# Output projection split in its own tiles, four homes for put-off residuals, and the second norm's root taken on 128x4 numbers

## The chip, the cores and the metric

One NeuronCore of a Trainium2 chip runs the whole program. The metric is device time in microseconds (us) of one execution; of several executions the median counts. The core has a matmul engine (PE, with its weight loads shown as PEld), a vector engine (DVE), an activation engine (ACT), a general engine (POOL, which here only issues DMAs) and SyncE (SP, which also issues DMAs). Each engine works through its own instructions in a fixed order and waits on semaphores of the others.

## The reference, cut to what matters

One layer of a decoder block over 2048 tokens of 1024 features. `g1`, `sh2`, `sc2`, `g2` are vectors made from the condition `c`.

```python
h = rms_norm(x, norm1_g) * (1 + sc1) + sh1
...  # gated linear attention (4 heads) and dilated attention (8 heads) on h
x = x + g1 * (concat(gla_out, attn_out) @ w_out)          # output projection
h = rms_norm(x, norm2_g) * (1 + sc2) + sh2                # the second norm
u = causal_depthwise_conv(h @ w_up, conv_w, conv_b)
a, b = split(u, 2)
x = x + g2 * ((silu(a) * b) @ w_down)                     # down projection

def rms_norm(x, g):
    return x * rsqrt(mean(x * x, axis=-1) + 1e-6) * g
```

## The kernel before

**Layout.** Tokens are cut into four chunks of T = 512 (c = 0 to 3). All activations lie with features on the 128 partitions and tokens along the row, so a chunk is KD = 8 tiles of 128x512. A matrix product is kept near fp32 by splitting both operands in a rounded part and a rest (`whi`, `wlo` for weights; `hhi`, `hlo` or `ghi`, `glo` for activations) and running three matmuls for each 128-block of the contraction (`mm3`: L314 hi·hi, L315 hi·lo, L316 lo·hi). Weights come by DMA on the POOL queue (L243) and are split by ACT (L248) and DVE (L249). GEMM results go to four PSUM banks (`psg`), everything else to the other four (`psa`).

**Order.** The program is traced by a tile framework whose scheduler, with an internal model of times, fixes the order on every engine. The source interleaves the mixing of chunk c+1 (`mix`: gated linear attention `gla`, then `attn` for four head pairs) with the GEMM chain of chunk c (`outproj(c)`, then `ffn(c)`); chunk 3's chain stands alone at the end.

**outproj(c).** The mixing has written its eight 128x512 results to DRAM, `y[0..7]` (`gla` the first four, `attn` of head pair hp the block 4+hp, L1051). `outproj` loads each back on the POOL queue into one of three "sq" tiles (L1067) and splits it (ACT L1076 hi, DVE L1077 lo). Eight column blocks follow (L1083 adds the residual and makes `x1`).

**Second norm.** ACT squares the eight `x1` tiles (L437), DVE adds them (L442). One fp32 matmul with a matrix of 1/1024 sums over partitions and spreads the mean over all of them (L456, 128x512). ACT takes Ln (L458) and Exp of -0.5 times it (L459), each with its own activation table; for chunk 0 four more DVE operations (L463 to L466) sharpen the root. Then for each feature block DVE multiplies (L476), ACT adds the shift and rounds (L478, `hhi`), DVE makes the rest (L480, `hlo`). The up-projection of `ffn` reads these.

**The put-off work.** Between the statistics and that last step `outproj` runs `self.tail`, GEMM work kept back so that PE is busy meanwhile. For c = 1 to 3 it is the last `down` group of the chunk before: eight column blocks of two 128-blocks, 48 matmuls. Each block reloads its residual from DRAM (L1148) into the tiles `y0` or `y1` (two slots each), adds (L1151) and stores (L1153 the result, L1155 the earlier partial `x1`). For c = 0 it is a piece of the input projection of chunk 3.

Of the kernel before, what the change touches and what calls it, by code (L numbers as in the profile page):

```python
# [10 lines left out]
F32 = mybir.dt.float32  # L11
# [3 lines left out]
ALU = mybir.AluOpType  # L15
# [129 lines left out]
class K:  # L145
# [174 lines left out]
    def ada_setup(self):  # L320
# [11 lines left out]
        self.eps = self.const.tile([P, 1], F32, name="eps")  # L332
        nc.vector.memset(self.eps, EPS)
        th = self.at.tile([P, 1024], F32, name="th", tag="v4", bufs=1)
        tanh = nc.scalar.activation(th, self.cond, AF.Tanh, scale=0.5)
# [88 lines left out]

    def norm_stats(self, src, step=False):

        acc = None
        for k in range(KD):
            acc = self.square(acc, src(k))
        return self.norm_end(acc, step)  # L430

# [12 lines left out]

    def norm_end(self, acc, step=False, split=False, more=()):
        nc = self.nc
# [12 lines left out]
        nc.scalar.activation(rstd, rstd, AF.Exp, scale=-0.5)  # L459
        if step:  # L460

            t = self.tmp.tile([P, T], F32, name="sq", bufs=3)
            nc.vector.scalar_tensor_tensor(t, ms, self.eps[:, 0:1], rstd, op0=ALU.add, op1=ALU.mult)  # L463
            nc.vector.tensor_tensor(t, t, rstd, op=ALU.mult)
            nc.vector.tensor_scalar(t, t, -3.0, -0.5, op0=ALU.add, op1=ALU.mult)
            nc.vector.tensor_tensor(rstd, rstd, t, op=ALU.mult)  # L466
        return rstd
# [200 lines left out]
    def gla(self, c, a):  # L668
# [106 lines left out]
        for s in range(2):  # L775
# [19 lines left out]
            yield  # L795
        nc.scalar.activation(ss, ss, AF.Ln, bias=self.eps, scale=1.0 / P)
        nc.scalar.activation(ss, ss, AF.Exp, scale=-0.5)
        ys = []
# [26 lines left out]
    def attn(self, c, hp, ready):  # L825
# [224 lines left out]
        nc.vector.tensor_tensor(st.rearrange("p (l r) -> p r l", r=16), O.rearrange("p (r l) -> p r l", r=16), st.rearrange("p (l r) -> p r l", r=16), op=ALU.add)  # L1050
        nc.sync.dma_start(D[c]["y"][4 + hp], st)  # L1051
        yield
# [9 lines left out]
    def outproj(self, c):  # L1062
        nc, A = self.nc, self.A
        hs = []
        for k in range(KD):
            t = self.tmp.tile([P, T], F32, name="sq", bufs=3)
            ld = self.dq.dma_start(t, self.D[c]["y"][k])  # L1067
            self.soon(ld)

            if c or k > 5:  # L1070
                hi, lo = (self.hp.tile([P, T], F32R, name=n) for n in ("hhi", "hlo"))
            elif k == 5:
                hi, lo = (self.up.tile([P, T], F32R, name=n, tag=n) for n in ("y0", "y1"))
            else:
                hi, lo = (self.gp.tile([P, T], F32R, name=n, tag=n) for n in ("ghi", "glo"))
            nc.scalar.copy(hi, t)  # L1076
            nc.vector.tensor_tensor(lo, t, hi.bitcast(F32), op=ALU.subtract)  # L1077
            hs.append((hi, lo))
        x1 = self.load_x(c)
        for cb in range(KD):  # L1080
            ps = self.pg()
            self.mm3(ps, self.weights("w_out", cb), hs)
            nc.vector.scalar_tensor_tensor(x1[cb], ps, self.mod[:, 16 + cb:17 + cb], x1[cb], op0=ALU.mult, op1=ALU.add)  # L1083
            yield
        self.x1[c] = x1
        rstd = self.norm_stats(lambda k: x1[k], not c)
        yield from self.tail
        self.h2[c] = self.norm_mod(lambda k: x1[k], rstd, self.G2, self.mod[:, 24:32], True)

# [43 lines left out]
    def down(self, c, gj, pgs):  # L1133
# [6 lines left out]
        for q in range(1024 // cols):  # L1140
            w = self.weights("w_down", gj * 4 + q)
            for cc in range(cols // P):
# [3 lines left out]
                if gj == 5 and defer:  # L1146
                    x1 = self.up.tile([P, T], F32, name="x1", tag=f"y{cb % 2}")
                    self.dq.dma_start(x1, self.D[c]["x1"][cb])  # L1148
# [182 lines left out]
```

## Time and profile before

| | |
|---|---|
| runs | 2580.99, 2582.28, 2589.22 us; median 2582.28 |
| profiled execution | 2578.59 us, of which the span of instructions is 2576.8 us |
| granted PE clock | 0.999 on average |
| busy, of the span | PE 2543.0 us, PEld 2096.0, DVE 1899.6, ACT 1264.6, POOL 449.2 |
| DMA | 408.47 MB, mean 159 GB/s |

The busy times show which engine the program leans on; the rows of single instructions show when each ran, how long it took, and behind "<-" in brackets what it had been waiting for. A waiting time is only worth something if PE is the engine that waits.

### The profile page before, as it was taken

Reading aid. Unit: us, or ns where it says so; the run is one execution under the profiler, and the core shown is the slowest. Engines: PE = TensorE matmul, PEld = TensorE weight load, DVE = VectorE, ACT = ScalarE, POOL = GpSimd, SP = SyncE. Lnnn points to the kernel's source line nnn. Section 1 sums busy time; section 2 is a strip of 40 time slices with the busy share of each in tenths; the row PEclk is TensorE's granted clock in tenths of the full one; section 3 lists DMA queues with packets and bytes.
Section 4 is the critical chain, followed back from the end, with each engine's and each line's share of the span. In section 5 each row is a group of like instructions: output and inputs, shape, how many; then the busy total and the mean of one; then the engine's idle time right before and its main releaser. Section 6 shows DMA issues by size and latency. Waiting matters only on the chain.

```text
span 2576.8 us, 49715 instructions
## 1 busy us (share of the span) xinstructions
PE 2543.0 (99%) x19458; PEld 2096.0 (81%) x19458; DVE 1899.6 (74%) x4111; ACT 1264.6 (49%) x2624; POOL 449.2 (17%) x818
## 2 busy tenths in 40 slices
PE   7999999999999999999999999999999999999999
PEld 4888888888788888887888888878888888788887
DVE  7678877867688766677977777689777775766665
ACT  5556655656454444454545444346444443433332
POOL 2333432323210000022100000310000003200001
PEclk9999999999999999999999999999999999999999
DMA  8876665756633444456334444743444535433232
GB/s 326 266 242 203 223 226 178 239 169 211 211 111 99 128 133 128 134 178 203 123 108 130 141 139 117 248 141 112 127 137 136 146 106 198 150 98 98 98 99 82
DMA packets 190622, 408.47 MB, mean 159 GB/s; under 512 B 48642, under 2 KB 89652, under 8 KB 189108
## 3 DMA queue, kind: packets, MB, share of 16 engines
q0 software_dynamic: 88416, 309.64, 37.0%
q1 hardware_dynamic: 101972, 95.65, 12.7%
q8 instruction: 154, 2.52, 0.4%
q14 instruction: 80, 0.66, 0.1%
HBM read 342.30 MB, written 62.91 MB: 157 GB/s over the span
## 4 chain that ended last, share of the span: by engine, by line
PE 94%; DVE 2%; issue 1%; DMA 1%; ACT 1%; POOL 1%; SPq 0%; POOLq 0%; DVEq 0%; ACTq 0%
PE psg L314 27%; PE psg L315 27%; PE psg L316 27%; PE psa L1028 2%; PE psa L902 2%; PE psa L876 2%; PE psa L709 2%; PE psa L1023 1%; PE psa L925 1%; PE psa L782 1%; PE psa L781 1%; PE psa L456 0%; PE psa L786 0%; PE psg L1200 0%; PE psa L1047 0%
## 5 line engine op out<-in xcount | busy, mean ns | idle before, releaser
L314 PE MATMUL psg<-hhi,whi 128*128 128x512 f32 x1968 | 771.2, 394 | 4.8 <-DVE x L1151 3.3
L315 PE MATMUL psg<-hlo,whi 128*128 128x512 f32 x1968 | 769.7, 392 | 2.2 <-DVE hlo L1077 1.9
L316 PE MATMUL psg<-hhi,wlo 128*128 128x512 f32 x1968 | 769.3, 392 | 0.7 <-DVE wlo L249 0.7
L248 ACT CAST whi<-wraw 128x1024 fp32r<-128x1024 f32 (+1 forms) x388 | 407.1, 1051 | 472.4 <-PE psg L315 360.7
L249 DVE TENSOR_TENSOR wlo<-wraw,whi 128x1024 fp32r<-128x1024 f32 (+1 forms) x388 | 474.5, 1223 | 202.7 <-ACT whi L248 194.4
L314 PEld LDWEIGHTS psg<-hhi,whi 128*128 128x128 f32 x1968 | 369.4, 188 | 84.9 <-ACT hhi L478 5.9
L316 PEld LDWEIGHTS psg<-hhi,wlo 128*128 128x128 f32 x1968 | 369.5, 188 | 78.6 <-DVE wlo L249 1.1
L315 PEld LDWEIGHTS psg<-hlo,whi 128*128 128x128 f32 x1968 | 369.6, 188 | 78.4 <-DVE hlo L1077 2.3
L314 PE MATMUL psg<-ghi,whi 128*128 128x512 f32 x744 | 294.6, 398 | 0.1
L315 PE MATMUL psg<-glo,whi 128*128 128x512 f32 x744 | 292.0, 393 | 0.4 <-DVE glo L1077 0.4
L316 PE MATMUL psg<-ghi,wlo 128*128 128x512 f32 x744 | 291.1, 391 | 0.7 <-DVE wlo L249 0.7
L243 POOL DMA_DIRECT2D wraw<-in_w_up_dram x176 | 96.4, 548 | 979.2 <-DVE wlo L249 814.8
L1151 DVE SCALAR_TENSOR_TENSOR x<-psg,mod,x 128x512 f32<-128x512 f32 x192 | 143.1, 748 | 112.4 <-PE psg L316 111.5
L314 PE MATMUL psg<-whi,hhi 128*128 128x512 f32 (+2 forms) x512 | 172.8, 342 | 2.9 <-ACT stg L582 1.4
L315 PE MATMUL psg<-wlo,hhi 128*128 128x512 f32 (+2 forms) x512 | 173.2, 339 | 0.0
L316 PE MATMUL psg<-whi,hlo 128*128 128x512 f32 (+2 forms) x512 | 173.0, 341 | 0.0
L314 PEld LDWEIGHTS psg<-ghi,whi 128*128 128x128 f32 x744 | 140.0, 188 | 31.3 <-issue 1.4
L316 PEld LDWEIGHTS psg<-ghi,wlo 128*128 128x128 f32 x744 | 139.9, 188 | 30.0 <-DVE wlo L249 1.1
L315 PEld LDWEIGHTS psg<-glo,whi 128*128 128x128 f32 x744 | 140.0, 188 | 28.9 <-DVE glo L1077 0.8
L1106 ACT ACTIVATE y<-psg,tables_sb 128x512 f32<-128x512 f32 x176 | 136.0, 775 | 3.0 <-PE psg L316 2.0
L1107 DVE SCALAR_TENSOR_TENSOR y<-psg,tables_sb,y 128x511 f32<-128x511 f32 x176 | 130.8, 744 | 2.8 <-ACT y L1106 2.7
L1108 DVE SCALAR_TENSOR_TENSOR y<-psg,tables_sb,y 128x510 f32<-128x510 f32 x176 | 130.8, 743 | 0.8
(271 smaller groups left out, 3604.0 us busy)
## 6 DMA issues: line engine op xcount, KB each, us to landing
wraw<-in_w_up_dram POOLq DMA_DIRECT2D x176, 512.0 KB, 3.8
wraw<-in_w_down_dram POOLq DMA_DIRECT2D x88, 512.0 KB, 3.8
wraw<-in_w_ch_dram POOLq DMA_DIRECT2D x44, 512.0 KB, 4.6
wada<-in_w_ada_dram POOLq DMA_DIRECT2D x64, 256.0 KB, 5.1
wraw<-in_w_tokw_dram POOLq DMA_DIRECT2D x32, 512.0 KB, 5.0
wraw<-in_w_out_dram POOLq DMA_DIRECT2D x32, 512.0 KB, 4.2
sq<-in_xT_dram POOLq DMA_DIRECT2D x48, 256.0 KB, 4.5
x<-x POOLq DMA_DIRECT2D x48, 256.0 KB, 5.6
```

The costliest lines, as they stand in the source:

```text
L243: ld = self.dq.dma_start(raw[:, :n], src)
L248: nc.scalar.copy(hi[:, :n], raw[:, :n])
L249: nc.vector.tensor_tensor(lo[:, :n], raw[:, :n], hi[:, :n].bitcast(F32), op=ALU.subtract)
L314: nc.tensor.matmul(ps, wh, hh, start=first and k == 0, stop=False, skip_group_check=shared)
L315: nc.tensor.matmul(ps, wh, hl, start=False, stop=False, skip_group_check=shared)
L316: self.lastmm = nc.tensor.matmul(ps, wl, hh, start=False, stop=k == n - 1, skip_group_check=shared)
L709: nc.tensor.matmul(sp[j:j + w, o + n * w:o + (n + 1) * w], kh[R, k0:k0 + w], qh[R, q0:q0 + w], start=True, stop=True)
L876: nc.tensor.matmul(at(i, hh, o, n)[H[z]], q(H[hh], i, z), key(H[hh], i, k0, n), start=True, stop=True, skip_group_check=True)
L1106: nc.scalar.activation(y, ps, AF.Identity, bias=self.cb[:, b:b + 1], scale=self.cw[:, 2, b:b + 1])
L1107: nc.vector.scalar_tensor_tensor(y[:, 1:], ps[:, :T - 1], self.cw[:, 1, b:b + 1], y[:, 1:], op0=ALU.mult, op1=ALU.add)
L1108: nc.vector.scalar_tensor_tensor(y[:, 2:], ps[:, :T - 2], self.cw[:, 0, b:b + 1], y[:, 2:], op0=ALU.mult, op1=ALU.add)
L1151: nc.vector.scalar_tensor_tensor(x1, ps, self.mod[:, 40 + cb:41 + cb], x1, op0=ALU.mult, op1=ALU.add)
```

## The change

Three edits, and two small ones beside them.

1. `outproj` loads `y[k]` straight into the tile that will hold the rest (`lo`), makes `hi` from it and subtracts in place; the "sq" tiles are no longer used there. The last block `y[7]` is taken from the tile in which `attn` made it, with no store and no reload.
2. The reloaded residuals of the put-off `down` group have four kinds of home: `y0`, `y1` for the first four column blocks, `ghi`, `glo` for the last four.
3. The second norm's root: four fp32 matmuls with the sum of squares as weights and one column of 1/1024 put the means of 512 tokens as 128x4 (tokens on partitions); ACT takes a square root of those, DVE the reciprocal; DVE multiplies the identity by it (128x512, four diagonal blocks), a ones matmul spreads it over the partitions, and ACT copies it to SBUF. The first feature block reads it in PSUM, the other seven read the copy. The scale 2^-20 in the square root cancels the factor 1/1024 that the second ones matmul brings in.
4. `gla`'s per-head norm takes square root and reciprocal in place of Ln and Exp.
5. One more constant, `eps20`.

Line numbers move: outproj load L1067 to L1086, hi L1076 to L1087, lo L1077 to L1088; root L456, L458, L459 to L435, L437, L438, L441, L443, L445; L476, L478, L480 to L485, L487, L489; put-off group L1148, L1151, L1153, L1155 to L1160, L1163, L1165, L1167; mask multiplies L709 to L718, copies L719 to L728, attention parts L729, L732 to L738, L741.

```diff
+        self.eps20 = self.const.tile([P, 1], F32, name="eps20")
+        nc.vector.memset(self.eps20, EPS * 2.0 ** -20)
...
-    def norm_stats(self, src, step=False):
+    def norm_stats(self, src):
         acc = None
         for k in range(KD):
             acc = self.square(acc, src(k))
-        return self.norm_end(acc, step)
+        ms = self.pa()
+        for b in range(4):
+            nc.tensor.matmul(ms[:, b:b + 1], acc[:, b * P:(b + 1) * P], self.ones.bitcast(F32)[:, 0:1], start=True, stop=True, skip_group_check=True)
+        r = self.tmp.tile([P, 4], F32, name="r4", bufs=1)
+        nc.scalar.activation(r, ms[:, 0:4], AF.Sqrt, bias=self.eps20, scale=2.0 ** -20)
+        nc.vector.reciprocal(r, r)
+        d = self.tmp.tile([P, T], F32, name="sq", bufs=3)
+        x = [P, 4, P]
+        nc.vector.tensor_tensor(d.rearrange("p (b n) -> p b n", b=4), self.C("id")[:, None, :].to_broadcast(x), r[:, :, None].to_broadcast(x), op=ALU.mult)
+        rstd = self.pa()
+        nc.tensor.matmul(rstd, self.ones.bitcast(F32), d, start=True, stop=True)
+        t = self.tmp.tile([P, T], F32, name="rstd", bufs=2)
+        nc.scalar.copy(t, rstd)
+        return [rstd] + [t] * (KD - 1)
...
-        if step:
-            t = self.tmp.tile([P, T], F32, name="sq", bufs=3)
-            nc.vector.scalar_tensor_tensor(t, ms, self.eps[:, 0:1], rstd, op0=ALU.add, op1=ALU.mult)
-            nc.vector.tensor_tensor(t, t, rstd, op=ALU.mult)
-            nc.vector.tensor_scalar(t, t, -3.0, -0.5, op0=ALU.add, op1=ALU.mult)
-            nc.vector.tensor_tensor(rstd, rstd, t, op=ALU.mult)
...
-        nc.scalar.activation(ss, ss, AF.Ln, bias=self.eps, scale=1.0 / P)
-        nc.scalar.activation(ss, ss, AF.Exp, scale=-0.5)
+        nc.scalar.activation(ss, ss, AF.Sqrt, bias=self.eps, scale=1.0 / P)
+        nc.vector.reciprocal(ss, ss)
...
-        nc.sync.dma_start(D[c]["y"][4 + hp], st)
+        if hp < 3:
+            nc.sync.dma_start(D[c]["y"][4 + hp], st)
+        else:
+            self.ylast = st
...
-            t = self.tmp.tile([P, T], F32, name="sq", bufs=3)
-            ld = self.dq.dma_start(t, self.D[c]["y"][k])
-            self.soon(ld)
...
+            t = self.ylast if k == KD - 1 else lo.bitcast(F32)
+            if k < KD - 1:
+                self.soon(self.dq.dma_start(t, self.D[c]["y"][k]))
             nc.scalar.copy(hi, t)
             nc.vector.tensor_tensor(lo, t, hi.bitcast(F32), op=ALU.subtract)
...
-        rstd = self.norm_stats(lambda k: x1[k], not c)
+        rstd = self.norm_stats(lambda k: x1[k])
         yield from self.tail
-        self.h2[c] = self.norm_mod(lambda k: x1[k], rstd, self.G2, self.mod[:, 24:32], True)
+        self.h2[c] = [self.norm_mod1(x1[k], k, rstd[k], self.G2, self.mod[:, 24:32], True) for k in range(KD)]
...
-                    x1 = self.up.tile([P, T], F32, name="x1", tag=f"y{cb % 2}")
+                    pool, tag = (self.up, "y") if cb < 4 else (self.gp, "g")
+                    x1 = pool.tile([P, T], F32, name="x1", tag=tag + (("0", "1") if cb < 4 else ("hi", "lo"))[cb % 2])
                     self.dq.dma_start(x1, self.D[c]["x1"][cb])
```

The scheduler's order changes with it. Names carry a buffer number behind the underscore.

DVE at the second norm of chunk 1, before, from the weight split ahead of the first multiply to the first rest tile (L476 multiply, L1151 residual add of the put-off group, L480 rest; L719, L732, L729 belong to the attention of chunk 2):

```order
1808 L249 TENSOR_TENSOR wlo_13374<-wraw_13371,whi_13373 128x1024
1809 L719 COPY_PREDICATED kt_12762<-masks_sb_404,psa_13186 128x128
1810 L476 SCALAR_TENSOR_TENSOR sq_13474<-x_12682,G2_111,rstd_13166 128x512
1811 L719 COPY_PREDICATED kt_12762<-masks_sb_404,psa_13186 128x128
1812 L476 SCALAR_TENSOR_TENSOR sq_13480<-x_12684,G2_111,rstd_13166 128x512
1813 L732 TENSOR_TENSOR pt_13257<-kt_12762,pt_13256 128x512
1814 L729 TENSOR_TENSOR pt_13285<-kt_12762 128x512
1815 L476 SCALAR_TENSOR_TENSOR sq_13486<-x_12686,G2_111,rstd_13166 128x512
1816 L719 COPY_PREDICATED kt_12762<-masks_sb_404,psa_13221 128x128
1817 L1151 SCALAR_TENSOR_TENSOR x1_13384<-psg_13377,mod_109,x1_13384 128x512
1818 L480 SCALAR_TENSOR_TENSOR hlo_13478<-sq_13474,mod_109,hhi_13476 128x512
```

The same engine and place now, from the residual add of the sixth put-off block on (L485 multiply, L1163 residual add):

```order
1817 L1163 SCALAR_TENSOR_TENSOR x1_13397<-psg_13390,mod_111,x1_13397 128x512
1818 L1163 SCALAR_TENSOR_TENSOR x1_13432<-psg_13425,mod_111,x1_13432 128x512
1819 L1163 SCALAR_TENSOR_TENSOR x1_13443<-psg_13436,mod_111,x1_13443 128x512
1820 L249 TENSOR_TENSOR wlo_13521<-wraw_13518,whi_13520 128x1024
1821 L485 SCALAR_TENSOR_TENSOR sq_13469<-x_12668,G2_113,psa_13160 128x512
1822 L485 SCALAR_TENSOR_TENSOR sq_13475<-x_12670,G2_113,rstd_13162 128x512
1823 L485 SCALAR_TENSOR_TENSOR sq_13481<-x_12672,G2_113,rstd_13162 128x512
1824 L728 COPY_PREDICATED kt_12748<-masks_sb_406,psa_13181 128x128
1825 L741 TENSOR_TENSOR pt_13252<-kt_12748,pt_13251 128x512
1826 L738 TENSOR_TENSOR pt_13280<-kt_12748 128x512
1827 L728 COPY_PREDICATED kt_12748<-masks_sb_406,psa_13216 128x128
1828 L489 SCALAR_TENSOR_TENSOR hlo_13473<-sq_13469,mod_111,hhi_13471 128x512
```

The multiplies stood ahead of the fifth residual add (row 1817 before); now all eight adds and one more weight split stand ahead of the first of them.

PE at the same place, before: the statistics' matmul L456, mask multiplies L709, and the sixth put-off block, with 18 put-off matmuls (rows 5621 to 5638) behind L456 and the first up-projection matmuls after them:

```order
5616 L456 MATMUL psa_13164<-rstd_13141,ones_99 128x512
5617 L709 MATMUL psa_13186<-pt_13094,pt_13093 32x32 x16
5618 L709 MATMUL psa_13186<-pt_13133,pt_13132 32x32 x16
5619 L709 MATMUL psa_13221<-pt_13094,pt_13093 32x32 x16
5620 L709 MATMUL psa_13221<-pt_13133,pt_13132 32x32 x16
5621 L314 MATMUL psg_13395<-ghi_12254,whi_12994 128x512
```

PE now: L435 stands at row 5616 in the place of L456, the same 18 matmuls follow it, and this is the end of them and what comes next:

```order
5634 L316 MATMUL psg_13436<-ghi_12389,wlo_12981 128x512
5635 L443 MATMUL psa_13160<-sq_13158,ones_99 128x512
5636 L718 MATMUL psa_13181<-pt_13080,pt_13079 32x32 x16
5637 L718 MATMUL psa_13181<-pt_13119,pt_13118 32x32 x16
5638 L718 MATMUL psa_13216<-pt_13080,pt_13079 32x32 x16
5639 L718 MATMUL psa_13216<-pt_13119,pt_13118 32x32 x16
5640 L314 MATMUL psg_13517<-hhi_13471,whi_13089 128x512
5641 L314 MATMUL psg_13567<-hhi_13471,whi_13166 128x512
5642 L314 MATMUL psg_13629<-hhi_13471,whi_13368 128x512
5643 L314 MATMUL psg_13691<-hhi_13471,whi_13520 128x512
5644 L315 MATMUL psg_13517<-hlo_13473,whi_13089 128x512
```

The mask multiplies moved from ahead of the put-off matmuls to behind them, the spreading matmul L443 stands between the two, and the up-projection opens four banks before it needs the first rest tile (in the old order it ran one bank, L314, L315, L316).

POOL, the DMA queue, at the output projection of chunk 0, before; the last two loads of `y` (blocks 6 and 7) stand behind loads of `x` and of keys:

```order
362 L1067 DMA sq_7357<-y0_123 128x512
363 L1067 DMA sq_7363<-y0_123 128x512
364 L1067 DMA sq_7369<-y0_123 128x512
365 L413 DMA x_7387<-in_xT_dram 128x512
...
374 L537 DMA k43_160<-o4_7289 128x512
375 L1067 DMA sq_7375<-y0_123 128x512
376 L1067 DMA sq_7381<-y0_123 128x512
```

Now, block 6 is loaded first of all, at row 349, and block 7 not at all:

```order
355 L1086 DMA glo_7341<-y0_125 128x512
356 L1086 DMA glo_7346<-y0_125 128x512
357 L1086 DMA glo_7351<-y0_125 128x512
...
363 L1086 DMA glo_7356<-y0_125 128x512
364 L1086 DMA glo_7361<-y0_125 128x512
...
372 L1086 DMA y1_7366<-y0_125 128x512
```

The load that comes last is now block 5's, eight rows behind the one before it.

More of the change, by code (lines that the diff above doesn't have):

```diff
@@ L423, in newton @@
         nc.vector.scalar_tensor_tensor(y, t, -3.0, y, op0=ALU.add, op1=ALU.mult)
-    def norm_stats(self, src, step=False):
+    def norm_stats(self, src):
+        nc = self.nc
         acc = None
@@ L443, in square, with norm_end @@
         return acc
-    def norm_end(self, acc, step=False, split=False, more=()):
+    def norm_end(self, acc, split=False, more=()):
         nc = self.nc
```

## The prediction

> **What bounds the kernel now.** I read the page's busy times and its chain first, then what PE waited for.
>
> ```profile
> PE 2543.0 (99%) x19458; PEld 2096.0 (81%) x19458; DVE 1899.6 (74%) x4111; ACT 1264.6 (49%) x2624; POOL 449.2 (17%) x818
> PE 94%; DVE 2%; issue 1%; DMA 1%; ACT 1%; POOL 1%; SPq 0%; POOLq 0%; DVEq 0%; ACTq 0%
> PE psa L456 <- ACT sq L1193: 14.1, 1, 14.1
> PE psg L314 <- DVE x L1151: 3.3, 2, 1.7
> PE psg L315 <- DVE hlo L1077: 1.9, 1, 1.9
> PE psg L314 <- ACT hhi L478: 1.5, 1, 1.5
> PE psg L316 <- DVE wlo L249: 1.4, 2, 0.7
> PE psa L709 <- DVE stage L1050: 0.7, 1, 0.7
> PE psg L315 <- DVE glo L1077: 0.4, 1, 0.4
> ```
>
> PE is the bound: 94% of the chain, and its longest wait, 14.1 us, is at the start and outside the change. The reader should see how little is left: the waits that name a step of the change (L1151, L1077, L478, L249) are 3.3 + 1.9 + 1.5 + 1.4 + 0.4 = 8.5 us, 0.33% of the span. Only work that PE itself gains or loses, and these waits, can move the time.
>
> The norm stall shows in the timeline. Chunk 1, from the statistics to the first up-projection matmul (start, length, engine, line):
>
> ```profile
> 1213.38 1.28 ACT L458 ACT_TABLE_LOAD   x1
> 1213.83 1.02 PE L456 MATMUL psa<-rstd,ones 128*128 128x512 f32 x2
> 1214.70 1.22 DVE L249 TENSOR_TENSOR wlo<-wraw,whi 128x1024 fp32r<-128x1024 f32 x1
> 1214.77 1.31 PE L709 MATMUL psa<-pt 64*32 64x32 f32 x128
> 1214.88 0.69 ACT L458 ACTIVATE rstd<-psa,eps 128x512 f32<-128x512 f32 x1 [0.21 <-PE psa L456]
> 1215.59 1.28 ACT L459 ACT_TABLE_LOAD   x1
> 1216.02 0.50 PE L314 MATMUL psg<-ghi,whi 128*128 128x512 f32 x1
> 1216.36 0.40 PE L315 MATMUL psg<-glo,whi 128*128 128x512 f32 x1
> 1216.59 0.39 PE L316 MATMUL psg<-ghi,wlo 128*128 128x512 f32 x1
> 1216.88 0.63 ACT L459 ACTIVATE rstd<-rstd 128x512 f32<-128x512 f32 x1
> 1217.55 0.75 DVE L476 SCALAR_TENSOR_TENSOR sq<-x,G,rstd 128x512 f32<-128x512 f32 x1 [1.42 <-ACT rstd L459]
> 1218.34 1.58 ACT L478 ACTIVATE hhi<-sq,mod 128x512 fp32r<-128x512 f32 x2 [0.82 <-DVE sq L476]
> 1219.68 0.69 DVE L729 TENSOR_TENSOR pt<-kt 128x512 f32<-128x512 f32 x1
> 1220.00 0.39 PE L316 MATMUL psg<-ghi,wlo 128*128 128x512 f32 x1
> 1220.28 0.75 DVE L476 SCALAR_TENSOR_TENSOR sq<-x,G,rstd 128x512 f32<-128x512 f32 x1
> 1220.94 0.29 DVE L719 COPY_PREDICATED kt<-masks_sb,psa 128x128 f32<-128x128 uint32 x1
> 1221.14 0.75 DVE L1151 SCALAR_TENSOR_TENSOR x<-psg,mod,x 128x512 f32<-128x512 f32 x1
> 1221.80 0.74 DVE L480 SCALAR_TENSOR_TENSOR hlo<-sq,mod,hhi 128x512 fp32r<-128x512 f32 x1
> 1222.03 0.47 PE L314 MATMUL psg<-hhi,whi 128*128 128x512 f32 x1 [1.64 <-DVE x L1151]
> 1222.60 0.50 PE L315 MATMUL psg<-hlo,whi 128*128 128x512 f32 x1
> ```
>
> Long rows start 0.23 us apart when PE is dense (1216.36, 1216.59), so after the last put-off matmul at 1220.00 the next could start at 1220.23. It starts at 1222.03: 1.80 us lost. The rounded tile it reads was long ready (L478 at 1218.34); it waited for a bank, freed by the residual add at 1221.14, which stood behind three multiplies in DVE's queue. L315 then starts 0.57 after L314 where 0.23 is normal: 0.34 more. So 2.14 us here. Chunk 2 is alike, and chunk 3 is shorter:
>
> ```profile
> 1717.45 0.39 PE L316 MATMUL psg<-ghi,wlo 128*128 128x512 f32 x1
> 1719.49 0.47 PE L314 MATMUL psg<-hhi,whi 128*128 128x512 f32 x1 [1.65 <-DVE x L1151]
> 2205.53 1.02 PE L456 MATMUL psa<-rstd,ones 128*128 128x512 f32 x2
> 2205.98 0.79 PE L314 MATMUL psg<-ghi,whi 128*128 128x512 f32 x1
> 2210.28 0.39 PE L316 MATMUL psg<-ghi,wlo 128*128 128x512 f32 x1
> 2212.14 0.47 PE L314 MATMUL psg<-hhi,whi 128*128 128x512 f32 x1 [1.47 <-ACT hhi L478]
> ```
>
> Chunk 2 loses 2.04 - 0.23 = 1.81, chunk 3 1.86 - 0.23 = 1.63, each with the same 0.34 taken behind it.
>
> **The change, part by part.**
>
> *Root with tokens on partitions, PE's share.* L443 is L456's matmul again (128x512, the same ones), so it replaces it one for one. New are four matmuls L435 with one column each, in all four chunks. Such a matmul takes two passes in the page's counting (L456: x2 for one), so eight, each with a load of 128x128 weights; the nearest rows are the 128x128 products of the gated attention, bound by the same loads:
>
> ```profile
> 649.40 0.28 PE L691 MATMUL psa<-tri,lh 128*128 128x128 f32 x1
> 649.51 0.28 PE L691 MATMUL psa<-tri,ll 128*128 128x128 f32 x1
> ```
>
> 0.11 us apart, so 8 x 0.11 = 0.9 us for each chunk, 3.6 us in all. Bounds: 0.45 if one pass does, 1.8 if the weight loads double; nothing hides it, since PE is dense on both sides. I take 0.9.
>
> *The chain behind it, chunk 1.* I place the new order on the old rows' times. L435 starts with L456, 1213.83, and ends at 1214.73; 18 put-off matmuls of 0.227 (1216.59 to 1220.00 in 15 steps) end at 1218.8. The root meanwhile: one table load, which can run ahead like that at 1213.38, a square root on four columns, and on DVE, behind L249 and the fifth add, reciprocal and one product, done by about 1217.5, so L443 does not wait. L443 takes 0.9 (L456: 1213.83 to 1214.77) and the moved mask multiplies 1.25 (1214.77 to 1216.02): PE is through at 1220.95. DVE has in its queue the residual adds of blocks 6 to 8, then L249, then the first multiply. The eighth add can begin when block 8 is done, about 1219.05, and takes 0.66 to the next start (1221.14 to 1221.80); L249 takes 1.14 (its 1.22 less the 0.08 by which DVE's rows overlap); so the first multiply starts about 1220.9. In the old rows L478 starts 0.79 after its multiply and needs 0.72 more: L314 at 1222.45, a stall of 1.5. The next rest tile stands behind two more multiplies (0.66 each), two L728 (0.20, as from 1220.94 to 1221.14) and two 128x512 products (0.60, 1219.68 to 1220.28): 0.66 x 3 + 0.4 + 1.2 = 3.6 after 1220.9, so L489 at 1224.5, and L315 0.80 later (1221.80 to 1222.60) at 1225.3. PE has four L314 in that time (0.9), which leaves 1225.3 - 1222.45 - 0.9 = 1.95. With 0.3 for a mask multiply that then catches its producer, 3.75 us against 2.14: 1.6 worse. Chunk 2 has the same orders: 1.5 worse.
>
> *Chunk 3.* Behind L456's place at 2205.53, L435 to 2206.43, tail to 2210.5, L443 to 2211.4. The eighth add at 2210.75, L249 behind it, first multiply 2212.5, L314 at 2214.05: 2.65; no attention is left, so the rest tile follows at 2214.5 and L315 at 2215.3 waits 0.35. Together 3.0 against 1.97: 1.0 worse. What is late in all three is the weight split and the adds ahead of the multiplies, not the root: the shorter root (one table, four columns) buys nothing, because L443 stands behind the put-off work anyway. The first block's reading the root in PSUM saves nothing either while the second block's copy runs on idle ACT.
>
> *Chunk 0's norm.* The put-off piece of the projection covers the chain; it pays L435, counted above. The four Newton operations on DVE go from beside that work: nothing.
>
> *Output projection.* The four waits around chunk 0's start:
>
> ```profile
> 664.75 0.50 PE L315 MATMUL psg<-glo,whi 128*128 128x512 f32 x1 [0.38 <-DVE glo L1077]
> 671.79 0.62 ACT L1076 CAST hhi<-sq 128x512 fp32r<-128x512 f32 x1 [3.06 <-DMA sq<-y]
> 676.71 0.50 PE L315 MATMUL psg<-hlo,whi 128*128 128x512 f32 x1 [1.89 <-DVE hlo L1077]
> 2177.74 0.50 PE L316 MATMUL psg<-hhi,wlo 128*128 128x512 f32 x1 [0.69 <-DVE wlo L249]
> L1067 POOL DMA_DIRECT2D sq<-y x32: 537/539/599, 629.8 to 2158.7; - x32
> ```
>
> The blocks 6 and 7 that came late at 671.79 are early now (one first in the queue, one never leaves SBUF), so 1.89 goes; 0.38 and a wait for L249 near 682 (0.7, the other of that row's two) go with the extra tiles. Late next is block 5, last in the queue, worth about 1.0 by the eight rows it stands behind. I take 3.3 (start to start) to 1.0, a gain of 2.3; bounds 0 and 3.3. The same L249 wait in chunk 3 (0.7, 0.86 start to start) should go, as the new order runs one bank to its end before the next and lets weights go one by one: -0.9. The 4 stores and 4 reloads of block 7, at 0.54 us of POOL each, were on no path of PE: nothing.
>
> *Twice the homes.* Reloads no longer wait for the stores of two blocks ago, so the adds come when their block is done. That frees the banks, the 1.64 of the old row at 1222.03, and is already in the sum, since I let the adds start at once.
>
> *Square root in gla.* DVE's reciprocal is 128 x a few numbers: nothing. But a square root needs a table of its own, and what follows must load its own again: the built program has 40 table loads for 30, the ten nearly all where the old trace is between 265 and 385 us, beside the projections of chunk 0. At 1.28 each they are 12.8 us of ACT, which was busy 49%; I take 0.5, bounds 0 and 12.8.
>
> The sum: 3.6 + 1.6 + 1.5 + 1.0 - 2.3 - 0.9 + 0.5 = +5.0 us on the profiled execution's 2578.59, 2583.6. The runs' median lies 3.69 above that execution, so 2587.3 against 2582.28; I say 2587.
>
> The Trainium skill (ScalarE: Activation LUTs, What ACT_TABLE_LOAD costs) states 1283 ns for the load and about 1380 more for a drain, 2.66 us a switch. The rows above agree with the load and not with the drain: L459 starts 1.29 after its table load, at 1216.88. By the page ten switches would be an estimated 26.6 us of ACT.
>
> **The rivals.**
>
> *The clock halves in the wider gap (slower).* Once in the middle of the program the clock was halved, right after a thin stretch (us, then PE, PEld, DVE, ACT, POOL busy, clock, DMA share, GB/s):
>
> ```profile
> 647.80:651.20 3.40, 1.85 (x42) 1.39 (x40) 2.71 (x4) 3.36 (x6) 0.54 (x1) 1.00 0.99 330
> 651.20:654.60 3.40, 3.28 (x38) 2.52 (x39) 3.40 (x7) 1.47 (x4) 0.54 (x1) 0.50 1.08 321
> 1219.90:1223.30 3.40, 1.66 (x7) 0.74 (x5) 3.40 (x7) 2.81 (x6) 1.08 (x2) 1.00 0.83 289
> ```
>
> Against it, the norm's stretch at 1219.90 is as thin and was not followed by a half clock. For it, my new order has about 0.9 us of PE work in the 4.3 us from 1220.9. Price: half of 3.4, 1.7 us a time, up to three times: +5.0 + 5.1 = +10, 2592. It decides from two times on. The Trainium skill (TensorE: Matmul & The Clock Gate, What's actually happening) says the clock falls after an idle window of about 3.4 us whose phase is free; the 3.4 us at 0.50 agree, and by that rule the three gaps would depend on how they fall on the windows.
>
> *Table loads reach PE (slower).* ACT rounds the weights (L248) for all of chunk 0's projections; if half of the ten loads end up ahead of a cast that PE waits for, +6.4, 2593; with all, +12.8. Against it: no L248 is in the waits list.
>
> *The waits simply go (faster).* If the adds and L249 do not delay the multiplies, because ACT's cast for that L249 and the eighth add finish before L443, then all 8.5 us of the named waits go, and with a freer DMA queue at 647 to 655 (share 0.99 to 1.08) the 0.7 of L1050 and the 1.7 of the half clock: with L435 at 0.9 to 0.45 a chunk, 10.9 - 3.6 = 7.3 to 10.9 - 1.8 = 9.1 gained, 2575 to 2573. Two thirds of that lies past 0.3%. It speaks against it that DVE's order is fixed with all of them ahead.
>
> *Nothing reaches PE but L435 and the first start.* The norm stalls stay at 2.1: +3.6 - 3.2 = +0.4, 2583. Here the new root does not do what it says: same stalls by another route.
>
> **How the numbers follow.** 0.3% of 2582 is 7.7 us, about what a measurement of this kernel can tell from no change. The forecast holds 0.46 (its own range 2583 to 2590), the nothing case 0.14, waits gone 0.15, half clock 0.16, table loads 0.09. Within 0.3% are the forecast less 0.04 at its upper end, the nothing case and a third of the waits-gone case: 0.61; faster 0.10; slower 0.29. The range goes from 2574, the gain case, to 2596, between the slow cases' 2592 and the 2600 (2587 + 12.8) of all loads on the path.
>
> **What would show it.** Right: L435's passes 0.11 apart behind L456's old place; L443 directly behind the put-off block with no wait; L314 after it waiting for ACT hhi L487 about 1.5 us, and L315 for DVE hlo L489 about 1.9 in chunks 1 and 2; no wait on L1088 over 1.2 us in chunk 0. Wrong: no PE wait on L487 or L489; a clock of 0.50 after the gaps; PE waiting for L248 between 265 and 385 us.

## The result, and the profile after

| | before | changed |
|---|---|---|
| runs | 7, 2580.24 to 2591.59 us | 7, 2590.05 to 2595.48 us |
| median | 2582.56 us | 2591.82 us |
| ratio | | 1.003, 95% interval 1.0019 to 1.0041 |
| span of the profiled execution | 2576.8 us | 2589.6 us |
| mean granted PE clock | 0.999 | 0.995 |

The changed kernel is slower, by 9.3 us between the medians, 0.36%, and the interval of the ratio lies clear of 1; the two profiled executions lie 12.8 us apart. Busy times, the chain, and what PE waited for (total us, times, longest):

```profile
PE 2550.7 (98%) x19490; PEld 2105.9 (81%) x19490; DVE 1904.2 (74%) x4124; ACT 1273.4 (49%) x2626; POOL 445.5 (17%) x814
PE 93%; DVE 3%; issue 1%; DMA 1%; ACT 1%; POOL 1%; SPq 0%; POOLq 0%; ACTq 0%
PE psg L314 <- ACT hhi L487: 4.3, 2, 2.8
PE psg L315 <- DVE hlo L489: 2.9, 2, 1.5
PE psa L700 <- ACT lh L694: 2.0, 1, 2.0
PE psg L315 <- DVE y L1088: 1.7, 1, 1.7
PE psa L532 <- ACT sqr L526: 1.2, 1, 1.2
PE psa L533 <- DVE sqr L527: 1.2, 1, 1.2
```

PE is busy 7.7 us longer for 32 more instructions of 0.1 us: the rest of that is PE running slower, which the clock shows below. The old waits on the residual add (L1151) and on blocks 6 and 7 (L1077) are gone; waits on the norm's own products, L487 and L489, stand in their place, and one on the rest tile of block 5 of the output projection (L1088).

The timeline of chunk 1's second norm, the stretch that the prediction laid out by hand:

```profile
1218.47 0.95 PE L435 MATMUL psa<-ones,rstd 128*128 128x1 f32 x8
1220.17 0.69 DVE L441 TENSOR_TENSOR sq<-consts_sb,r 128x512 f32<-128x512 f32 x1
1223.27 0.40 PE L316 MATMUL psg<-ghi,wlo 128*128 128x512 f32 x1
1223.51 1.02 PE L443 MATMUL psa<-sq,ones 128*128 128x512 f32 x2
1223.71 0.75 DVE L1163 SCALAR_TENSOR_TENSOR x<-psg,mod,x 128x512 f32<-128x512 f32 x1 [0.62 <-PE psg L316]
1224.46 1.32 PE L718 MATMUL psa<-pt 64*32 64x32 f32 x128
1224.59 1.22 DVE L249 TENSOR_TENSOR wlo<-wraw,whi 128x1024 fp32r<-128x1024 f32 x1
1225.73 0.74 DVE L485 SCALAR_TENSOR_TENSOR sq<-x,G,psa 128x512 f32<-128x512 f32 x1
1227.28 1.34 PE L314 MATMUL psg<-hhi,whi 128*128 128x512 f32 x4 [1.51 <-ACT hhi L487]
1229.32 1.41 DVE L489 SCALAR_TENSOR_TENSOR hlo<-sq,mod,hhi 128x512 fp32r<-128x512 f32 x2
1230.12 0.79 PE L315 MATMUL psg<-hlo,whi 128*128 128x512 f32 x1 [1.50 <-DVE hlo L489]
```

L435 is eight passes, and the next matmul starts 0.80 later. The root's last operand was ready at 1220.17 + 0.69 = 1220.9, but the spreading matmul L443 ran at 1223.51, behind the put-off work. It ended at 1223.51 + 1.02 = 1224.53; the first multiply started 1.20 later, at 1225.73, behind the eighth add (L1163) and the weight split (L249). Then PE waits 1.51 and 1.50 us. The four L314 behind the first wait take 1.34 us as a group, and the L315 lasts 0.79 where 0.50 was usual after a wait. The windows say why (us, then PE, PEld, DVE, ACT, POOL busy, clock, DMA share, GB/s):

```profile
1224.40:1227.80 3.40, 1.89 (x131) 1.68 (x131) 3.27 (x6) 2.04 (x4) 1.08 (x2) 1.00 0.70 230
1227.80:1231.20 3.40, 1.90 (x6) 1.09 (x6) 3.40 (x8) 2.67 (x5) 0.00 (x0) 0.56 0.38 145
1231.20:1234.60 3.40, 3.40 (x10) 2.63 (x9) 3.40 (x7) 1.53 (x4) 0.00 (x0) 0.50 0.00 0
```

After the thin stretch the clock is halved for 6.8 us, and the second half of that is full of matmuls at half speed. Behind the norms of chunks 2 and 3 it is halved for 3.4 us each:

```profile
1729.40:1732.80 3.40, 2.43 (x6) 1.97 (x7) 3.40 (x9) 2.52 (x4) 0.00 (x0) 0.58 0.07 27
2225.10:2228.50 3.40, 3.40 (x10) 2.65 (x9) 3.40 (x6) 1.92 (x3) 0.00 (x0) 0.53 0.12 43
```

The other new loss is early, in chunk 0. ACT and PE rows around it:

```profile
264.96 1.28 ACT L805 ACT_TABLE_LOAD   x1
292.54 1.28 ACT L534 ACT_TABLE_LOAD   x1
294.54 1.28 ACT L535 ACT_TABLE_LOAD   x1
298.41 0.61 ACT L526 CAST sqr<-sq 128x512 fp32r<-128x512 f32 x1
299.07 0.50 PE L532 MATMUL psa<-sqr,blk 128*128 128x512 f32 x1 [1.21 <-ACT sqr L526]
301.04 0.51 PE L533 MATMUL psa<-sqr,blk 128*128 128x512 f32 x1 [1.17 <-DVE sqr L527]
```

Before, none of these loads was there; the same places read (Ln of the first `gla` norm, Ln and Exp of the query norm, with no load between them):

```profile
264.59 0.30 ACT L796 ACTIVATE gss<-gss,eps 128x8 f32<-128x8 f32 x1
288.73 0.67 ACT L525 ACTIVATE sq<-psa,eps 128x512 f32<-128x512 f32 x1
289.43 0.63 ACT L526 ACTIVATE sq<-sq 128x512 f32<-128x512 f32 x1
```

The code preloads one table set, `natural_log_exp_and_others`, and the Ln and Exp ahead of 264 us use it together. The square root at 266 us needs another, and behind it each Ln and the Exp that follows it load a table of their own: eleven loads from 264 to 314 us, where the trace before has none.

To put numbers on stretches I numbered the GEMM matmuls (L314 to L316; 9696 in every kernel) and read, at the time of each in the trace before, how much later the same number starts in another trace. The difference over a stretch is what the stretch costs; the few places where the order inside the stretch differs are bridged by its ends, which lie in stretches of equal order.

| us over the kernel before | to 250 | gla root 250-330 | outproj 0, 640-760 | norm 1, 1180-1310 | norm 2, 1700-1850 | norm 3, 2200-2250 | end |
|---|---|---|---|---|---|---|---|
| changed | 0.4 | 3.6 | 1.1 | 3.2 | 3.1 | 3.7 | 12.8 |
| changed again (e5) | 3.8 | 3.5 | -1.3 | 2.8 | 4.4 | 3.2 | 14.3 |
| changed again (e11) | 0.7 | 3.6 | -0.6 | 3.1 | 3.0 | 3.6 | 11.7 |

The table leaves out what lies between its stretches, so its rows do not add up to the end. The norms and gla's root repeat within 1.4 us; the beginning and the output projection do not, for a reason that comes at the end. The two repeats were expected so:

> The changed kernel itself, unaltered, as the base for the runs beside it on this chip. Both theories: 1.003 to 1.0045 of the kernel before, half clocks behind each second norm of chunks 1 to 3 and at 302.

> The changed kernel unaltered, beside e9 on the same chip: 1.003 to 1.0045 of the kernel before.

They measured 2592.14 us, ratio 1.0032 (1.002 to 1.0045), and 2590.98 us, 1.003 (1.0021 to 1.0039). The clock was halved behind all three norms in both; the half clock expected at 302 us was there in e11 and not in e5, which had one at 197 instead.

### The profile page after: what moved, and what is told of

The parts are those of the page before. It is cut to its first block, busy times and chain, and to the rows that moved or that the text cites. A ratio compares the mean times of both kernels' runs of the same rounds, so it can differ in the third digit from the quotient of the medians.

```text
span 2589.6 us, 49764 instructions
## 1 busy us (share of the span) xinstructions
PE 2550.7 (98%) x19490; PEld 2105.9 (81%) x19490; DVE 1904.2 (74%) x4124; ACT 1273.4 (49%) x2626; POOL 445.5 (17%) x814
## 3 DMA queue, kind: packets, MB, share of 16 engines
q8 instruction: 154, 2.52, 0.4%
## 4 chain that ended last, share of the span: by engine, by line
PE 93%; DVE 3%; issue 1%; DMA 1%; ACT 1%; POOL 1%; SPq 0%; POOLq 0%; ACTq 0%
PE psg L314 27%; PE psg L315 27%; PE psg L316 26%; PE psa L1037 2%; PE psa L911 2%; PE psa L885 2%; PE psa L718 1%; PE psa L1032 1%; PE psa L934 1%; PE psa L791 1%; PE psa L790 1%; DVE sq L485 0%; PE psa L795 0%; PE psg L1212 0%; PE psa L533 0%
## 5 line engine op out<-in xcount | busy, mean ns | idle before, releaser
L314 PE MATMUL psg<-hhi,whi 128*128 128x512 f32 x1968 | 776.5, 396 | 4.3 <-ACT hhi L487 4.3
L315 PE MATMUL psg<-hlo,whi 128*128 128x512 f32 x1968 | 771.6, 393 | 2.9 <-DVE hlo L489 2.9
L316 PE MATMUL psg<-hhi,wlo 128*128 128x512 f32 x1968 | 771.9, 393 | 0.0
L248 ACT CAST whi<-wraw 128x1024 fp32r<-128x1024 f32 (+1 forms) x388 | 407.0, 1050 | 456.3 <-PE psg L315 367.7
L249 DVE TENSOR_TENSOR wlo<-wraw,whi 128x1024 fp32r<-128x1024 f32 (+1 forms) x388 | 474.7, 1224 | 211.6 <-ACT whi L248 201.1
L314 PEld LDWEIGHTS psg<-hhi,whi 128*128 128x128 f32 x1968 | 370.8, 189 | 84.1 <-ACT hhi L487 5.4
L315 PEld LDWEIGHTS psg<-hlo,whi 128*128 128x128 f32 x1968 | 371.5, 189 | 79.8 <-DVE hlo L489 4.4
L316 PEld LDWEIGHTS psg<-hhi,wlo 128*128 128x128 f32 x1968 | 371.2, 189 | 78.1 <-issue 0.7
L314 PE MATMUL psg<-ghi,whi 128*128 128x512 f32 x744 | 294.2, 397 | 0.0
L315 PE MATMUL psg<-glo,whi 128*128 128x512 f32 x744 | 292.5, 393 | 0.0
L316 PE MATMUL psg<-ghi,wlo 128*128 128x512 f32 x744 | 291.3, 391 | 0.0
L1163 DVE SCALAR_TENSOR_TENSOR x<-psg,mod,x 128x512 f32<-128x512 f32 x192 | 143.5, 749 | 114.8 <-PE psg L316 113.8
L314 PE MATMUL psg<-whi,hhi 128*128 128x512 f32 (+2 forms) x512 | 172.8, 342 | 2.5 <-ACT stg L591 1.7
L315 PE MATMUL psg<-wlo,hhi 128*128 128x512 f32 (+2 forms) x512 | 173.3, 340 | 0.0
L316 PE MATMUL psg<-whi,hlo 128*128 128x512 f32 (+2 forms) x512 | 172.8, 340 | 0.0
L314 PEld LDWEIGHTS psg<-ghi,whi 128*128 128x128 f32 x744 | 140.2, 189 | 29.8 <-issue 0.5
L316 PEld LDWEIGHTS psg<-ghi,wlo 128*128 128x128 f32 x744 | 140.1, 188 | 29.0
L315 PEld LDWEIGHTS psg<-glo,whi 128*128 128x128 f32 x744 | 140.2, 188 | 28.4 <-issue 0.7
```

Source lines behind the costliest of these rows:

```text
L248: nc.scalar.copy(hi[:, :n], raw[:, :n])
L249: nc.vector.tensor_tensor(lo[:, :n], raw[:, :n], hi[:, :n].bitcast(F32), op=ALU.subtract)
L314: nc.tensor.matmul(ps, wh, hh, start=first and k == 0, stop=False, skip_group_check=shared)
L315: nc.tensor.matmul(ps, wh, hl, start=False, stop=False, skip_group_check=shared)
L316: self.lastmm = nc.tensor.matmul(ps, wl, hh, start=False, stop=k == n - 1, skip_group_check=shared)
L1163: nc.vector.scalar_tensor_tensor(x1, ps, self.mod[:, 40 + cb:41 + cb], x1, op0=ALU.mult, op1=ALU.add)
```

## The experiments

**Gla's root alone, both ways.** e1 takes it out of the changed kernel, e2 puts it alone into the kernel before.

```diff
-        nc.scalar.activation(ss, ss, AF.Sqrt, bias=self.eps, scale=1.0 / P)
-        nc.vector.reciprocal(ss, ss)
+        nc.scalar.activation(ss, ss, AF.Ln, bias=self.eps, scale=1.0 / P)
+        nc.scalar.activation(ss, ss, AF.Exp, scale=-0.5)
```

> The changed kernel with gla's root again as Ln and Exp, all else as changed. Theory (the square root drops the activation table that holds Ln and Exp together, so ACT loads ten tables more around 265 to 385 us and PE waits twice for ACT and DVE at 297 to 301 us, with a half clock behind): no L534 or L535 table load before 385 us, no PE wait on L526 or L527 near 299, no half clock there, 4.0 us less than the changed kernel, about 2588. Rival (the waits at 299 come from the new order of the output projection or the norm, not from tables): they stay, and the time stays within 1 us of the changed kernel.

> The kernel before with only gla's root as square root and reciprocal. Theory: the whole 4.0 us of the stretch at 299 appears here alone, 2586.5, and nothing else after 400 us. Rival (ten table loads are hidden on an ACT that is half idle): within 1 us of the kernel before.

e2: 2585.64 us, ratio 1.0012 (1.0003 to 1.0021). Its stretch from 250 to 330 costs 3.5 us, the rest of the program together nothing (3.2 us at the end), and its list of waits has two new ones of over 1 us:

```profile
PE psa L523 <- ACT sqr L517: 1.2, 1, 1.2
PE psa L524 <- DVE sqr L518: 1.2, 1, 1.2
```

The rival, that ten loads hide on a half idle ACT, has fallen. e1: 2588.48 us, ratio 1.0029 (1.0019 to 1.0038); its stretch costs -0.7 where the changed kernel's costs 3.6, so the 4 us are gone there in the trace, but the median does not show it clearly against the changed kernel's 1.003: the intervals overlap, and this run alone would not have settled it. Its trace also loses 1.5 us at 366 us, where PE waits 1.09 us on `gla` (L817); the changed kernel's trace has no such wait there.

**The parts taken apart.** e3 is the kernel before with the output projection's part and the homes; e7 with the homes alone; e4 with the new second-norm root alone (parts 1, 2; part 2; part 3 of the diff above, unaltered).

> The kernel before with the output projection's part and the residuals' homes, but the old second-norm root and the old gla root. Theory (the new root, not the homes, puts the stalls at the second norm): the order on DVE has the fifth residual add ahead of the multiplies, so PE's wait on that add (3.3 us in two) goes; the waits on L1077 go in part; 3 to 6 us less than before, about 2578. Rival (the homes let all adds and a weight split crowd ahead of the multiplies, whatever the root): the stalls of the changed kernel, 1.5 and 1.5 us at each norm with a half clock, appear here too, 2587 or more.

> The kernel before with the residuals' homes alone. Theory (the homes move the fifth residual add ahead of the multiplies and end the wait for the bank, the output projection's part gives little): the norm stretches gain about 1.2 us each as with both parts, 3.5 us in all, 2578. Rival (the gain of 7 us of both came from the output projection's operands): within 1 us of the kernel before.

> The kernel before with only the second norm's root changed. Theory: the norm stretches of chunks 1 to 3 lose about what the changed kernel loses there (3.7, 3.0 and 3.5 us, of it 0.8 each for L435 and some 1.7 for each half clock), so 2592. Rival (crowding by the homes does it): the stretches lose 0.8 each for L435 and no more, about 2585.

| kernel | median us | ratio to before (95%) | outproj 0 | norm 1 | norm 2 | norm 3 |
|---|---|---|---|---|---|---|
| e3, operands and homes | 2575.03 | 0.9978 (0.9966 to 0.999) | -1.8 | -1.2 | -0.7 | -0.6 |
| e7, homes | 2579.68 | 0.9986 (0.9977 to 0.9995) | -0.1 | -0.5 | -0.6 | -0.6 |
| e4, new root | 2599.88 | 1.007 (1.0056 to 1.0083) | -0.2 | 5.0 | 7.1 | 4.4 |

So the first two parts help and the new root does all the harm at the norm; the rival of e3, that the homes crowd the multiplies, has fallen. e7's gain at the norms is half of what I had set (1.7 us instead of 3.5), though its median lies 4.1 us under the kernel before's (2579.68 against 2583.74), so the trace accounts for less than half of it. e3's trace gains 4.6 us by its end; the 1.8 us at chunk 0's output projection stand against 2.1 us lost between 330 and 640, whose cause is open. And the new root alone costs more than the whole change, 18.1 us by the medians (2599.88 against 2581.74 on that chip) and 19.6 in the profile: with two homes the residual reload comes late, and the add that waits for it stands ahead of the first multiply on DVE. From e4's timeline (L1167 residual add, L492 multiply, L494 rounding):

```profile
1222.69 1.41 DVE L1167 SCALAR_TENSOR_TENSOR x<-psg,mod,x 128x512 f32<-128x512 f32 x2 [3.41 <-DMA x<-x]
1225.14 0.74 DVE L492 SCALAR_TENSOR_TENSOR sq<-x,G,psa 128x512 f32<-128x512 f32 x1
1226.70 0.73 PE L314 MATMUL psg<-hhi,whi 128*128 128x512 f32 x2 [2.35 <-ACT hhi L494]
```

The homes, worth 1.7 us at the norms beside the old root, take a wait of 3.4 us out of the new one.

**Is it the gap that halves the clock?** e6 puts work that nobody reads in front of the first up-projection matmul (cut; `self.fill` is an operand of the put-off group):

```diff
                         ps = self.pg()
-                        self.mm3(ps, self.weights("w_up", b), h2)
+                        w = self.weights("w_up", b)
+                        if c and not gi and f == 0 and half == 0:
+                            for _ in range(12):
+                                nc.tensor.matmul(ps, w[0][0], self.fill, start=True, stop=True)
+                        self.mm3(ps, w, h2)
```

> The changed kernel with 12 extra matmuls of 128x512, whose result is overwritten, ahead of the first up-projection matmul of chunks 1, 2 and 3 (36 x 0.227 = 8.2 us more PE work). Theory (the clock halves because PE stands idle in the norm's gaps, at a cost of about 6.5 us over three chunks): with the gaps filled the clock stays at 1.00 behind them; the extra work lies in idle time but for some 1 us a chunk, so 3 to 4 us less than the changed kernel although it does more. Rival (the half clocks come with the load or at fixed times, not from the gap): they stay, and the time is the same or up to 8 us more.

```profile
1224.27 1.99 PE L1118 MATMUL psg<-ghi,whi 128*128 128x512 f32 x8
1226.09 1.02 PE L443 MATMUL psa<-sq,ones 128*128 128x512 f32 x2
1228.29 1.20 PE L1118 MATMUL psg<-ghi,whi 128*128 128x512 f32 x4
1232.16 0.50 PE L315 MATMUL psg<-hlo,whi 128*128 128x512 f32 x1 [1.63 <-DVE hlo L489]
```

```profile
1229.40:1232.80 3.40, 1.77 (x8) 1.16 (x8) 3.40 (x8) 2.67 (x4) 0.00 (x0) 1.00 0.21 84
1232.80:1236.20 3.40, 3.40 (x17) 2.79 (x16) 3.40 (x7) 1.53 (x4) 0.00 (x0) 1.00 0.00 0
```

The clock stays at 1.00 behind all three norms, although one gap of 1.6 us is left, and the mean granted clock of its five executions is 0.997 or 0.998, where e5's five on the same chip have 0.994 to 0.997: the half clocks came from the idle time and not from the place or the load. The time is that of the changed kernel, 2591.16 us, 1.0034 (1.0022 to 1.0047), with 8.2 us more work on PE. The 3 to 4 us less that I had expected did not come: the scheduler put eight of the twelve ahead of L443 and so made the root, and all behind it, 1.8 us later. That this is the whole reason was not tested.

**Is it the place of the spreading matmul?** e9 is the changed kernel with one dependency more: the first matmul of the seventh put-off block waits for L443 (here L444). Cut to its main part (`spread` is L444, `firstmm` the first matmul of the block just traced):

```diff
-        yield from self.tail
+        for i, _ in enumerate(self.tail):
+            if c and i == 6:
+                self.tie(self.firstmm, self.spread)
+            yield
```

> The changed kernel with one edit: the spreading matmul of the root is put ahead of the last two blocks of the put-off group (its operand is ready at 1220.9, the matmul ran at 1223.5). Theory (the place of that matmul, behind all put-off work, makes the multiplies late and opens the gaps, and the gaps halve the clock): PE's waits on L487 go, the half clocks behind the norms go, the three norm stretches come from 4.2, 3.8 and 3.7 us over the kernel before down to about 1 each, so 8 us less than the changed kernel, 2584. Rival (residual adds and weight split ahead of the multiplies on DVE, as the prediction had it, or L435 itself): less than 2 us gained.

2580.43 us, ratio 0.9986 (0.9977 to 0.9995), beside the changed kernel's 2590.98 on the same chip: 10.6 us less from one added dependency, and 3.6 us better than expected. Its norm 1 in the timeline, and the windows there:

```profile
1217.62 0.95 PE L436 MATMUL psa<-ones,rstd 128*128 128x1 f32 x8
1220.16 1.10 PE L444 MATMUL psa<-sq,ones 128*128 128x512 f32 x2
1221.92 0.75 DVE L486 SCALAR_TENSOR_TENSOR sq<-x,G,psa 128x512 f32<-128x512 f32 x1 [1.04 <-ACT rstd L446]
1225.29 0.61 PE L314 MATMUL psg<-hhi,whi 128*128 128x512 f32 x2
1226.31 0.50 PE L316 MATMUL psg<-hlo,whi 128*128 128x512 f32 x1 [0.40 <-DVE hlo L490]
```

```profile
1220.00:1223.40 3.40, 3.32 (x135) 2.34 (x135) 2.25 (x5) 1.29 (x3) 0.58 (x2) 1.00 0.92 271
1223.40:1226.80 3.40, 3.00 (x13) 2.17 (x13) 3.40 (x7) 2.67 (x5) 0.00 (x0) 1.00 0.19 69
```

The wait of the first multiply ends with the copy of the root, no longer with adds and a split; the L314 comes without a wait, the remaining gap is 0.4 us, the clock stays. The norms cost -0.5, 0.9 and 0.0 us. L435, unaltered here, does not carry the loss. The adds and the weight split are not cleared by this run: as soon as the matmul stood earlier, the scheduler moved the multiplies ahead of the last two adds and of the split on DVE. In the changed kernel's order the first multiply stands behind both, so an earlier L443 alone could not have brought it forward. What the run shows is the worth of the matmul's place together with the order that the scheduler makes of it; how much either gives alone stays open.

**Put together.** e8 is e3 with one thing more, in chunk 0 only: the output projection multiplies block 5, which is split last, at the end. e10 is the changed kernel with gla's old root, the early spreading matmul and the same block order. e12 repeats e8.

```diff
-            self.mm3(ps, self.weights("w_out", cb), hs)
+            ks = range(KD) if c else (0, 1, 2, 3, 4, 6, 7, 5)
+            w = self.weights("w_out", cb)
+            self.mm3(ps, [w[k] for k in ks], [hs[k] for k in ks])
```

> Output projection's part and homes, old roots, and in chunk 0 the output projection multiplies block 5, the last to be split, after blocks 6 and 7. Theory (PE's wait of 1.7 us on the rest tile of block 5 near 675 us is only its place in the contraction): the wait goes, 1 to 2 us less than with both parts alone, 2573.5. Rival (what is won there is lost at the next wait): same as with both parts, 2575.

> Output projection's part with block 5 last, homes, the new second-norm root with the early spreading matmul, and gla's root as before. Theory: the new root costs 0.8 for L435 in each of four chunks and else runs like the old one, so 3 us more than with the old root (e8), 2577. Rival (a root that is ready earlier lets the multiplies start earlier and beats the old root): 2573 or less.

> The kernel of e8 unaltered, beside e10 on the same chip: 0.9955 to 0.998 of the kernel before.

e8 2573.95 us, 0.9965 (0.9953 to 0.9978), and again 2574.42, 0.9958 (0.9946 to 0.9971): the fastest kernel here, about 0.4% ahead of the kernel before. The wait on block 5's rest (1.7 us on L1079 in e3) is not in its list; of the medians only 1.1 us separates it from e3, and the intervals overlap, so what the block order adds is not settled. e10 is 2576.68, 0.9971 (0.9961 to 0.9982): by the medians the new root, well placed, costs 2.3 us more than the old one beside it on that chip, about the 3 that L435 was set at, though the intervals overlap; its rival, a root that beats the old one, did not show.

## Why the prediction was right, and where it was not

The time, 2591.8, lies in the range (2574 to 2596), on the slower side of the 2587 named. Between its own cases the outcome is the one called "the clock halves in the wider gap", priced at 2592 and given 0.16; the forecast without it was given 0.46. The median is 0.36% up where no change that can be told from noise was held likeliest, at 0.61: the side of +0.3% that had 0.29.

The range held because it had been drawn wide enough for the slow cases, not because the sum was right. In the trace the 5.0 us of the sum became 12.8: 3.2 more at the three norms, 3.1 more at gla's root and 2.5 more at chunk 0's output projection with its L435, less 1.0 elsewhere. Of the signs named in advance, L443 directly behind the put-off block and the waits on L487 and L489 came; L1088 held PE for 1.7 us where 1.2 was the limit, and a sign of being wrong, the clock of 0.50 after the gaps, came behind all three norms.

*PE's share of the root.* Set at 0.9 us a chunk; measured 0.80 from the start of L435 to the next matmul.

*The chain behind it.* The hand-laid order held almost to the row in chunk 1: L314 waits 1.51 (predicted 1.5), L315 1.50 (1.95), and the first multiply starts 2.2 us behind the start of L443 (predicted 2.1). In chunk 2 the first wait, 1.64, is booked on the last mask multiply (L718) ahead of L314; in chunk 3 L314 waits 2.76 (2.65). Predicted in all for the three norms with L435: 2.5, 2.4 and 1.9; measured 3.2, 3.1 and 3.7, 10.0 instead of 6.8. What the term left out is the halved clock behind each gap, which stood among the rivals at 1.7 a time. Chunk 3 was the most undersized: its wait was as laid out, and the 1.8 more is about one half clock.

*The cause given for it.* "What is late in all three is the weight split and the adds ahead of the multiplies, not the root" is the step that failed, in its second half. The adds and the split stood where the order said, and in that order they held the first multiply 1.20 us beyond the end of L443. But the order was taken as given: the root's last matmul, 2.6 us ready before it ran, is what the late multiplies hang on, since with it two blocks earlier (e9) the scheduler puts them ahead of the last adds and of the split, and the gap closes. The half sentence behind it, that L443 stands behind the put-off work, was the thing to follow.

*Homes.* Right that they free the banks: the wait on the fifth add is gone, and beside the old root they gain (e7). I treated that gain as inside the sum without a number; at the norms it is 1.7 us with the old root, and with the new one about 6.5 (16.5 in e4 against the changed kernel's 10.0).

*Output projection.* Chunk 0 was set at -2.3, with L435 -1.4; the executions with that part gave anything from -1.9 (e1) to 1.5 (e6), the changed kernel's three 1.1, -1.3 and -0.6. Block 5 was indeed the next late one, 1.7 us instead of 1.0. The spread goes with the wait for `lh` ahead of it, 2.0 us in the row of L700 above against 0.6 before, and with a clock halved behind that for 6.8 us, for 3.4 as before, or not at all (e1). Chunk 3's 0.9 came, as 1.3 (lag at 2100 to 2200: 10.4 to 9.1).

*Gla's root.* Set at 0.5 within bounds of 0 and 12.8; measured 3.5 (e2). The mechanism, ten more loads of 1.28 us in that stretch, was named; that PE would wait for a query cast (L526) behind two of them was not looked for in the order, only L248 was. The drain that the Trainium skill adds to each load (ScalarE: Activation LUTs, What ACT_TABLE_LOAD costs) did not show here either: L534's load at 292.54 is followed by its activation at 293.83, 1.29 later.

## What to carry to other kernels

Where a dense matmul stream has a dependent chain with filler work behind it, look at where the chain's own matmuls stand among the filler: one matmul queued behind it all makes the chain as long as the filler, however short its other steps are. When it is moved, look again at the order of the other engines, for the scheduler may change that too. Count a PE gap of one or two microseconds at more than its length, because a halved clock may follow it. And before a new activation function is brought in, see which set is loaded and who lives in it: the cost falls on the others, far from the edit.

## What the runs showed of the hardware that was not expected

The half clock comes in pieces of 3.4 us, one to three behind a gap (10.24 us behind chunk 2's norm in e4), and the same gap does not always bring it. At one place early in the program PE waits for a staging copy. In the kernel before:

```profile
194.06 0.39 PE L314 MATMUL psg<-whi,hhi 128*128 128x272 f32 x1 [1.42 <-ACT stg L582]
```

The same matmul in e5, the changed kernel:

```profile
196.46 0.39 PE L314 MATMUL psg<-whi,hhi 128*128 128x272 f32 x1 [1.86 <-ACT stg L591]
```

And in e11, the same kernel again:

```profile
194.71 0.39 PE L314 MATMUL psg<-whi,hhi 128*128 128x272 f32 x1 [2.64 <-ACT stg L591]
```

Only the middle one was followed by a half clock, and that execution was 3.8 us behind the kernel before at 250 us, e11 only 0.7. So length alone does not decide.

What else counts can be read from when the half clocks start: in each trace they lie whole steps of 3.413 us apart. In the changed kernel's they start at 303.17, 654.75, 1228.19, 1729.94 and 2224.88 us, which is 103, 168, 147 and 145 steps. The Trainium skill (TensorE: Matmul & The Clock Gate, What's actually happening) says that the gate looks at free-running windows of about 3.4 us; that agrees with these steps, and it would make part of the spread between executions of one kernel a matter of where its gaps fall. An idle window, as the prediction gives the rule, was not needed: in the step ahead of each of these five PE was busy for 0.96 to 2.24 of 3.41 us.

Cut along these steps, e11's gap of 2.64 us is shared between two of them; in the emptier one PE is busy 1.59 of 3.41 us, in e5's 1.55. e6's gap behind chunk 1's norm is shared too, with 2.54 and 2.66 busy. But the busy share alone does not decide either: in e6 a step with 1.77 busy behind chunk 2's norm brought no half clock, and in e11 one with 2.52 busy, at 654 us, did. What decides between them is open.
